# Moving a block inversion from VectorE to GpSimd, and the loads, queries and memory scores around it, in a hybrid decoder trunk

## The chip, the cores and the metric

The kernel runs on one core of a Trainium2 chip. The metric is device time in microseconds of one launch. The kernel before takes 1113.31 us as the median of three runs (1112.72 to 1115.05). The engines are named as in the profile: PE (TensorE), DVE (VectorE), ACT (ScalarE), POOL (GpSimd) and SP (SyncE, which in this kernel only issues transfers). Each engine runs its own instructions strictly in the order in which they stand in its queue; engines wait for each other through semaphores.

## The reference, cut to what matters

Two layers over 512 positions of width 1024. Layer 0 is a gated DeltaNet layer with 6 heads of 128 and a memory attention with 4 heads of 64 over 256 fixed tokens; layer 1 is sliding-window attention with the same kind of memory attention; each layer ends in a SwiGLU block. The change lies in layer 0 only:

```
proj = h @ w_in                                   # h: rms_norm(x)
qkv  = silu(causal_depthwise_conv(proj[..., :2304], conv_w))
q, k = l2_normalize(...), l2_normalize(...)       # 6 heads of 128
lower = where(strict, (k*beta) @ k^T * decay, 0)  # per head and chunk of 64
sol   = triangular_solve(I + lower, [v*beta, k*beta*exp(g)])
intra = q @ k^T * decay
state = state*g_last + k_g^T @ (u - w @ state); o = q_g @ state + intra @ v_new
mem_o = softmax(mem_q @ mem_k^T / 8) @ mem_v
x     = x + concat([gated_norm(o), mem_o]) @ w_out
```

The kernel uses chunks of 128 rather than 64 positions: 4 chunks for each of 6 heads, so 24 lower triangular matrices of 128 x 128 that have to be inverted.

## The kernel before, in words

Activations lie transposed, with 128 features on the partitions and the 512 positions along the row. Each f32 matrix product is made of three passes of a faster kind: weights and activations are both split into a high and a low part (`whi`, `wlo`, `h`, `l`), and `mm3` (L198) issues high by high, high by low and low by high. One projection, that is one tile of 128 outputs of `w_in`, is thus 8 x 3 = 24 matmuls of 128x512 into one PSUM bank `pj`. Its weights come by one SP transfer of 512 KB into `wraw` (`load`, L174 to L178, two buffers), ACT copies them to `whi` (L138) and DVE subtracts to get `wlo` (L151). A weights load therefore waits until the weights two before it have been split.

The function `gdn` is layer 0's mixer. After the keys it forms, per head and chunk, the strictly lower matrix `N`, and sends its 32x32 diagonal blocks (24 matrices x 4 blocks = 96) to DRAM and back, so that they lie as 96 partitions of 1024 numbers. `base_inverse` (L778) inverts all 96 blocks at once by forward substitution: 31 rounds, each a product of a column by a row (`btmp`) and a subtraction from the inverse (`big`), on rectangles of r x w with w = 1 to 31 and r = 32 - w. Each of these 62 instructions needs the one before it. Then ACT writes a turned copy, SP stores both to DRAM (`basex`, `basext`), and SP loads them back as blocks (`X`, 4 loads; `Tt`, 4 loads) into the places that `solve` works on. `solve` starts on PE after the queries and joins the blocks to inverses of 128.

While that runs, PE works on the queries. Six projections give the queries of heads 0 to 5, three by three, in `memory` and the loop after it (L694 to L708). Each is followed by a causal convolution (`conv_tile`: one ACT copy, three DVE instructions into `qv`), an ACT silu, and `query` (L682): four 128x128 products with the keys into a bank `g`, a DVE product into `DT`, a DVE product into `gcr`, an ACT square into `sq`, and an SP store of `sq` to DRAM (`q`). The tile `sq` has one buffer, so the square of a head waits until the store of the head before has landed.

The memory attention of layer 0 is done in two halves (m = 0, 1). `scores` makes eight products of 64x256 (16 matmuls in the profile) into banks `g` and `sc`, DVE takes the maxima, ACT the exponentials into `sm`. `weigh` scales `sm`, turns it on PE into banks `g`, ACT copies these into `pf` (one buffer), and PE multiplies `pf` by the memory values into a bank `sc`. There are two banks `g`, three `sc` and three `pj`.

A scheduler sets the order on each engine from the program's order, the data and its own reckoning of durations; `nosync(a, b)` only makes it put a behind b, without a wait on the chip.

Of the kernel before, what the change touches and what calls it, by code (L numbers as in the profile page):

```python
# [9 lines left out]
F32 = mybir.dt.float32  # L10
# [3 lines left out]
ALU = mybir.AluOpType  # L14
# [4 lines left out]
P = 128  # L19
T = 512  # L20
D = 1024
KD = D // P
H = 6
NC = 4
# [6 lines left out]
BASE = 32  # L31
# [3 lines left out]
LN_EXP = "natural_log_exp_and_others"  # L35
# [49 lines left out]
class Builder:  # L85
# [466 lines left out]
    def gdn(self, gp):  # L552
        nc, a, tc = self.nc, self.a, self.tc
# [29 lines left out]
        for h in range(H):  # L583
            ps = self.begun[h] if h < 3 else None
# [11 lines left out]
            if h == 3:  # L596
                late = self.copied
# [22 lines left out]
        for h in range(H):  # L620
            d = DT[h]
# [36 lines left out]
        self.use(LN_EXP)  # L658
        scores = [self.scores(gp, qm[0], self.memK[0], False)]
        memory_queries(1)  # L660
        X, every_t = self.base_inverse(gp, base_in, known)
        Tt = [every_t[:, h * NC:(h + 1) * NC, :] for h in range(H)]
        for i in range(NH):
            h, c = divmod(i, NC)
            self.copy(kg[h][:, c, :], kg[h][:, c, :], scale=f[:, 2, i:i + 1])

        def memory(m, first, late):

            if m:
                self.use(LN_EXP)  # L670
                scores.append(self.scores(gp, qm[m], self.memK[m], False))
            ps = self.normed(first)
            steps = self.projected(a["win"][first + 1], self.h)
            nxt = [next(steps) for _ in range(2)]
            self.ahead = self.last
            while late:
                query(*late.pop(), self.ahead)
            self.weigh(gp, scores[m], self.memV, m, mq[m], None)
            nxt.extend(steps)
            return ps, nxt[-1]  # L680

# [15 lines left out]
        late = []  # L697
        for h0 in (0, 3):
            ps = memory(h0 // 3, h0, late)
            ts = [self.conv_tile(h0 + n, self.t(gp, [P, T], F32, "qv", 5), ps[n] if n < 2 else None) for n in range(3)]  # L700
            behind = self.last
            self.use(SILU_SIN)
            for h, t in zip(range(h0, h0 + 3), ts):
                self.fn(t, t, AF.Silu)
                if h == 2:
                    late.append((h, t))
                else:
                    query(h, t, behind)  # L708
# [65 lines left out]
    def base_inverse(self, gp, base_in, after):  # L774

        nc = self.nc
        n = NH * NB
        e = BASE * BASE  # L778
        whole = self.t(gp, [P, 4 * T], F32, "big")
        big = lambda i: whole[:n, i * e:(i + 1) * e].rearrange("p (a b) -> p a b", b=BASE)  # L780
        L = big(0)
        nc.sync.dma_start(L.rearrange("p a b -> p (a b)"), base_in.rearrange("n b e -> (n b) e"))
        X = big(1)
        Xf = X.rearrange("p a b -> p (a b)")
        clear = lambda out, value: self.nosync(nc.vector.memset(out, value).ins, after)
        clear(Xf, 0.0)
        clear(Xf[:, ::BASE + 1], 1.0)
        for j in range(BASE - 1):
            r, w = BASE - 1 - j, j + 1
            tmp = self.t(gp, [n, 256], F32, "btmp", 2)[:, :r * w].rearrange("p (i m) -> p i m", m=w)  # L790
            self.tt(nc.vector, tmp, L[:, j, j + 1:].unsqueeze(2).to_broadcast([n, r, w]),
                    X[:, j, :w].unsqueeze(1).to_broadcast([n, r, w]), ALU.mult)
            self.tt(nc.vector, X[:, j + 1:, :w], X[:, j + 1:, :w], tmp, ALU.subtract)
        Xt = big(0)
        self.copy(Xt, X.rearrange("p i m -> p m i"))
        outs = []
        for nm, src in (("basex", X), ("basext", Xt)):
            d = self.t(self.dpool, [NH, NB, BASE * BASE], F32, nm)
            nc.sync.dma_start(d.rearrange("n b e -> (n b) e"), src.rearrange("p a b -> p (a b)"))
            outs.append(d)  # L800
        X64 = self.t(gp, [P, NH, 2 * BASE], F32, "X64")
        clear(X64, 0.0)
        for b in range(NB):
            s = slice(b * BASE, (b + 1) * BASE)
            o = b % 2 * BASE
            nc.sync.dma_start(X64[s, :, o:o + BASE], outs[0][:, b, :].rearrange("n (i m) -> i n m", m=BASE))
        Tt = self.t(gp, [P, NH, P], F32, "Tt")
        clear(Tt, 0.0)
        for b in range(NB):
            s = slice(b * BASE, (b + 1) * BASE)  # L810
            nc.sync.dma_start(Tt[s, :, s], outs[1][:, b, :].rearrange("n (m i) -> m n i", i=BASE))
        return X64, Tt

    def solve(self, gp, N, X64, Tt):
# [93 lines left out]
        return new  # L908


    def scores(self, pool, q, kk, win, sinks=None):

        nc = self.nc
        own = "pt" in self.pbufs
# [5 lines left out]
        for n0 in range(0, NC, 2):  # L920
# [5 lines left out]
            for n in (n0, n0 + 1):  # L926
                ks = slice((n - 1) * P if n else 0, (n + 1) * P) if win else slice(0, ML)
                c0 = P if win and n == 0 else 0
                for b in range(2):
                    self.ahead = self.mm(ps[b][:, n - n0, c0:], q[half[b], n * P:(n + 1) * P], kk[half[b], ks])  # L930
                    if self.valued is not None:

                        self.nosync(self.ahead, self.valued)
                        self.valued = None
            for b in range(2):
                i = b * NC + n0
                if win:
# [813 lines left out]
```

## Time and profile before

| what | value |
|---|---|
| median of three runs | 1113.31 us |
| the profiled execution | 1112.83 us |
| its span, first to last instruction | 1111.1 us |
| busy share of PE, DVE, ACT, POOL | 99%, 84%, 63%, 10% |
| queries, weighing and solve of layer 0 | about 119 to 195 us of the span |
| granted clock | 0.998 |

The profiled execution lies 0.48 us under the median, and 1.73 us of it lie outside the span. A timeline row gives the start in the span, the length, the engine, the line, the operation, the tiles (out<-in), the shapes and how many equal instructions it joins; behind it, in brackets, the engine's idle time before it and what ended that. PE's rows overlap, since matmuls are pipelined: there the distance from one start to the next is the cost. A line can be that of a helper: L144 is every matmul, L151 every two-operand DVE or POOL instruction, L138 every ACT copy.

### The profile page before, as it was taken

The numbers are of one execution on the slowest core, as the hardware profiler recorded it, in microseconds if no ns is written. First come the engines' busy times: TensorE is split into PE (matmuls) and PEld (weight loads), VectorE is DVE, ScalarE is ACT, GpSimd is POOL, SyncE is SP. The second block draws the span as 40 slices with busy tenths as digits, with TensorE's granted clock in tenths as the row PEclk, the third lists the DMA queues.
The fourth block names the chain that finished last, engine by engine and source line by source line (L and its number), as shares of the span: only waits on it lengthen the run. The fifth ranks groups of instructions, "written<-read, shape, count | busy, mean of one in ns | idle before, by whom it ended". The sixth has DMA issues, their size and how long they took to land.

```text
span 1111.1 us, 21262 instructions
## 1 busy us (share of the span) xinstructions
PE 1100.6 (99%) x7957; PEld 998.9 (90%) x7957; DVE 937.0 (84%) x1890; ACT 697.2 (63%) x1470; POOL 105.9 (10%) x129
## 2 busy tenths in 40 slices
PE   9999999999999999999999999999999999999997
PEld 8888778877899999999998777788899999999996
DVE  7685977667899999999997977839999999998964
ACT  7588674466566656665565654866667466655644
POOL 0000000000011121112110000000111111121101
PEclk9999999999999999999999999999999999999999
DMA  8244352234567787778753321114677776778632
GB/s 320 98 151 142 114 142 82 90 98 145 150 173 183 189 190 191 179 184 199 191 147 99 117 74 40 58 58 142 159 176 192 189 195 184 186 198 203 148 86 90
DMA packets 81146, 165.36 MB, mean 149 GB/s; under 512 B 18588, under 2 KB 20148, under 8 KB 81044
## 3 DMA queue, kind: packets, MB, share of 16 engines
q1 hardware_dynamic: 64436, 133.87, 38.0%
q0 software_dynamic: 16320, 29.89, 16.5%
q8 instruction: 62, 1.02, 0.4%
q14 instruction: 40, 0.33, 0.1%
q10 hardware_dynamic: 288, 0.26, 0.1%
HBM read 156.98 MB, written 7.01 MB: 148 GB/s over the span
## 4 chain that ended last, share of the span: by engine, by line
PE 92%; DVE 5%; ACT 1%; issue 1%; DMA 0%; SPq 0%; DVEq 0%; ACTq 0%
PE g L144 54%; PE pj L144 26%; PE sc L144 6%; PE qk L144 3%; PE pt L144 2%; PE pt L148 1%; DVE wlo L151 1%; PE g L148 1%; DVE l L154 1%; DVE big L151 1%; DVE x L151 1%; DMA early<-in_early 0%; DVE fu L151 0%; DVE qv L154 0%; DVE btmp L151 0%
## 5 line engine op out<-in xcount | busy, mean ns | idle before, releaser
L138 ACT ACTIVATE whi<-wraw 128x512 fp32r<-128x512 f32 (+2 forms) x357 | 250.6, 711 | 161.4 <-PE g L144 66.3
L151 DVE TENSOR_TENSOR wlo<-wraw,whi 128x512 fp32r<-128x512 f32 (+2 forms) x357 | 280.5, 793 | 36.8 <-ACT whi L138 31.8
L144 PE MATMUL g<-T,whi 128*128 128x256 f32 x1280 | 228.3, 279 | 0.0
L144 PE MATMUL g<-h,wlo 128*128 128x256 f32 (+1 forms) x780 | 222.7, 285 | 0.6 <-DVE wlo L151 0.6
L144 PE MATMUL g<-l,whi 128*128 128x256 f32 (+1 forms) x780 | 222.6, 285 | 0.0
L144 PE MATMUL g<-h,whi 128*128 128x256 f32 (+1 forms) x780 | 222.4, 285 | 0.0
L144 PEld LDWEIGHTS g<-T,whi 128*128 128x128 f32 x1280 | 194.9, 188 | 0.5 <-DVE fu L154 0.5
L144 PE MATMUL pj<-h,whi 128*128 128x512 f32 (+1 forms) x460 | 182.0, 398 | 0.0
L144 PE MATMUL pj<-l,whi 128*128 128x512 f32 (+1 forms) x460 | 180.4, 393 | 0.4 <-DVE l L154 0.3
L144 PE MATMUL pj<-h,wlo 128*128 128x512 f32 (+1 forms) x460 | 179.8, 391 | 0.0
L144 PE MATMUL g<-T,wlo 128*128 128x256 f32 x640 | 178.5, 279 | 0.0
L144 PEld LDWEIGHTS g<-h,wlo 128*128 128x128 f32 x780 | 146.6, 188 | 2.8 <-DVE wlo L151 1.1
L144 PEld LDWEIGHTS g<-l,whi 128*128 128x128 f32 x780 | 146.6, 188 | 1.9
L144 PEld LDWEIGHTS g<-h,whi 128*128 128x128 f32 x780 | 146.6, 188 | 1.8
L144 PEld LDWEIGHTS g<-T,wlo 128*128 128x128 f32 x640 | 120.3, 188 | 0.0
L144 PEld LDWEIGHTS pj<-h,whi 128*128 128x128 f32 x460 | 86.4, 188 | 20.7 <-issue 4.1
L144 PEld LDWEIGHTS pj<-h,wlo 128*128 128x128 f32 x460 | 86.5, 188 | 18.0 <-issue 0.9
L144 PEld LDWEIGHTS pj<-l,whi 128*128 128x128 f32 x460 | 86.5, 188 | 17.8 <-DVE l L154 1.2
L138 ACT ACTIVATE whi<-ws 128x512 fp32r<-128x512 f32 x112 | 70.1, 626 | 38.9 <-PE g L144 36.8
L151 DVE TENSOR_TENSOR wlo<-ws,whi 128x512 fp32r<-128x512 f32 x112 | 77.1, 689 | 2.9 <-ACT whi L138 2.9
L1394 POOL DMA_DIRECT2D ws<-in_wgu x40 | 35.1, 878 | 414.6 <-DVE l L154 203.9
L138 ACT ACTIVATE fs<-g 128x256 f32<-128x256 f32 x168 | 61.5, 366 | 1.1 <-PE g L144 0.7
(398 smaller groups left out, 1929.6 us busy)
## 6 DMA issues: line engine op xcount, KB each, us to landing
wraw<-in_wgu SPq DMA_DIRECT2D x48, 512.0 KB, 4.0
ws<-in_wgu SPq DMA_DIRECT2D x80, 256.0 KB, 3.6
ws<-in_wgu POOLq DMA_DIRECT2D x80, 256.0 KB, 4.9
wraw<-in_win SPq DMA_DIRECT2D x26, 512.0 KB, 4.0
wraw<-in_wgu SPq DMA_DIRECT2D x40, 256.0 KB, 5.4
wraw<-in_wout SPq DMA_DIRECT2D x16, 512.0 KB, 3.4
ws<-in_wdn SPq DMA_DIRECT2D x32, 256.0 KB, 5.7
wraw<-in_wdn SPq DMA_DIRECT2D x16, 512.0 KB, 3.8
```

Source lines behind the costliest of these rows:

```text
L138: self.copied = self.nc.scalar.activation(out, in_, AF.Copy, **kw).ins
L144: return self.nc.tensor.matmul(out, lhsT, rhs, start=start, stop=stop, skip_group_check=more).ins
L148: return self.nc.tensor.transpose(out, in_, self.ident[:k, :k]).ins
L151: return eng.tensor_tensor(out=out, in0=a, in1=b, op=op).ins
L154: return self.nc.vector.scalar_tensor_tensor(out=out, in0=in0, scalar=scalar, in1=in1, op0=op0, op1=op1).ins
L1394: nc.gpsimd.dma_start(s1, a22, accum_op=ALU.add)
```

## The change

Five things are altered, all in layer 0.

1. The 62 instructions of the block inversion, the turned copy and the two stores go to POOL; before, they stood on DVE, ACT and SP.
2. `base_inverse` ends with the stores. The clearing of `X64` and `Tt` and the eight block loads become a function of their own, `base_blocks`, which is called after the convolution of head 5's query has been issued; its loads stay on SP, and are put behind the load of the sixth query's weights.
3. The second half's `scores` come right behind the first half's weighing, and no longer behind the queries of heads 0 and 1. So ACT no longer changes its table of functions twice in between.
4. The queries of heads 0 and 1 (before: only that of head 2) are put off into the second `memory`: behind the first three of the eight steps of head 3's projection. Head 2's stays behind two steps of head 4's.
5. `scores` gets an argument `after`, which no call uses.

```diff
-        X, every_t = self.base_inverse(gp, base_in, known)
-        Tt = [every_t[:, h * NC:(h + 1) * NC, :] for h in range(H)]
+        outs = self.base_inverse(gp, base_in, known)
...
         def memory(m, first, late):
 
+            steps = self.projected(a["win"][first], self.h)
             if m:
-                self.use(LN_EXP)
-                scores.append(self.scores(gp, qm[m], self.memK[m], False))
-            ps = self.normed(first)
+                nxt = [next(steps) for _ in range(3)]
+                while len(late) > 1:
+                    query(*late.pop(0), self.last)
+            ps = list(steps)[-1]
             steps = self.projected(a["win"][first + 1], self.h)
             nxt = [next(steps) for _ in range(2)]
             self.ahead = self.last
             while late:
                 query(*late.pop(), self.ahead)
             self.weigh(gp, scores[m], self.memV, m, mq[m], None)
+            if not m:
+                scores.append(self.scores(gp, qm[1], self.memK[1], False))
             nxt.extend(steps)
             return ps, nxt[-1]
...
             ps = memory(h0 // 3, h0, late)
-            ts = [self.conv_tile(h0 + n, self.t(gp, [P, T], F32, "qv", 5), ps[n] if n < 2 else None) for n in range(3)]
+            conv = lambda n, ps: self.conv_tile(h0 + n, self.t(gp, [P, T], F32, "qv", 5), ps)
+            ts = [conv(n, ps[n]) for n in range(2)]
+            ts.append(conv(2, None))
             behind = self.last
+            if h0:
+                X, every_t = self.base_blocks(gp, outs, known, self.loaded)
+                Tt = [every_t[:, h * NC:(h + 1) * NC, :] for h in range(H)]
             self.use(SILU_SIN)
             for h, t in zip(range(h0, h0 + 3), ts):
                 self.fn(t, t, AF.Silu)
-                if h == 2:
+                if h < 3:
                     late.append((h, t))
...
-            self.tt(nc.vector, tmp, L[:, j, j + 1:].unsqueeze(2).to_broadcast([n, r, w]),
+            self.tt(nc.gpsimd, tmp, L[:, j, j + 1:].unsqueeze(2).to_broadcast([n, r, w]),
                     X[:, j, :w].unsqueeze(1).to_broadcast([n, r, w]), ALU.mult)
-            self.tt(nc.vector, X[:, j + 1:, :w], X[:, j + 1:, :w], tmp, ALU.subtract)
+            self.tt(nc.gpsimd, X[:, j + 1:, :w], X[:, j + 1:, :w], tmp, ALU.subtract)
         Xt = big(0)
-        self.copy(Xt, X.rearrange("p i m -> p m i"))
+        nc.gpsimd.tensor_copy(Xt, X.rearrange("p i m -> p m i"))
         outs = []
         for nm, src in (("basex", X), ("basext", Xt)):
             d = self.t(self.dpool, [NH, NB, BASE * BASE], F32, nm)
-            nc.sync.dma_start(d.rearrange("n b e -> (n b) e"), src.rearrange("p a b -> p (a b)"))
+            nc.gpsimd.dma_start(d.rearrange("n b e -> (n b) e"), src.rearrange("p a b -> p (a b)"))
             outs.append(d)
+        return outs
+
+    def base_blocks(self, gp, outs, known, after):
+
+        nc = self.nc
+        clear = lambda out, value: self.nosync(nc.vector.memset(out, value).ins, known)
         X64 = self.t(gp, [P, NH, 2 * BASE], F32, "X64")
         clear(X64, 0.0)
         for b in range(NB):
             s = slice(b * BASE, (b + 1) * BASE)
             o = b % 2 * BASE
-            nc.sync.dma_start(X64[s, :, o:o + BASE], outs[0][:, b, :].rearrange("n (i m) -> i n m", m=BASE))
+            self.nosync(nc.sync.dma_start(
+                X64[s, :, o:o + BASE], outs[0][:, b, :].rearrange("n (i m) -> i n m", m=BASE)).ins, after)
...
-            nc.sync.dma_start(Tt[s, :, s], outs[1][:, b, :].rearrange("n (m i) -> m n i", i=BASE))
+            self.nosync(nc.sync.dma_start(
+                Tt[s, :, s], outs[1][:, b, :].rearrange("n (m i) -> m n i", i=BASE)).ins, after)
         return X64, Tt
```

What this makes of the order shows at three places. The first is SP's queue around the block loads. `wraw` are weights loads, `q` the stores of the squares of heads 0, 1 and 2, in this order. Before:

```order
L177 DMA wraw_1826<-in_win 128x1024
L695 DMA q_314_1647<-sq_1645 128x512
L177 DMA wraw_2096<-in_win 128x1024
L695 DMA q_317_1659<-sq_1657 128x512
L799 DMA basex_1442<-big_1344 96x1024
L799 DMA basext_1444<-big_1344 96x1024
L806 DMA X_288_1446<-basex_1442 32x24x32 x4
L811 DMA Tt_1452<-basext_1444 32x24x32 x4
L695 DMA q_337_1749<-sq_1747 128x512
```

And now, with `wraw_1813` the sixth query's weights and `wraw_2094` the first ones for the values:

```order
L177 DMA wraw_1714<-in_win 128x1024
L177 DMA wraw_1813<-in_win 128x1024
L820 DMA X_350_1848<-basex_1442 32x24x32 x4
L826 DMA Tt_1854<-basext_1444 32x24x32 x2
L698 DMA q_325_1686<-sq_1684 128x512
L826 DMA Tt_1854<-basext_1444 32x24x32
L698 DMA q_328_1697<-sq_1695 128x512
L826 DMA Tt_1854<-basext_1444 32x24x32
L177 DMA wraw_2094<-in_win 128x1024
L698 DMA q_335_1736<-sq_1734 128x512
```

The stores of heads 0 and 1 stood ahead of the block loads; now all three stores and the next weights load stand behind the first six or more of the eight block loads.

The second place is ACT's queue around the three squares (`sq`), with the waits that the built program holds; `DMAHW1` and `DMAHW3` on the second and third square are the landings of the stores of the square before, `DMAHW5` that of `wraw_2094`. Before, from the copy of head 1's convolution to the silu of head 2:

```order
L138 ACTIVATE qv_1595<-pj_1519,gains_67 128x512 [waits DMAHW7_49,PE_49]
L132 ACTIVATE qv_1595<-qv_1595 128x512 [waits DVE_49,Activation_49]
L138 ACTIVATE qv_1600<-pj_1607,gains_67 128x512 [waits PE_49]
L693 ACTIVATE sq_1657<-qv_1595 128x512 [waits DMAHW3_49,Activation_49]
L138 ACTIVATE whi_1828<-wraw_1826 128x1024 [waits DMAHW2_49]
L138 ACTIVATE big_1344<-big_1344 96x1024 [waits DVE_49,Pool_49]
L132 ACTIVATE qv_1600<-qv_1600 128x512 [waits DVE_49,Activation_49]
```

And now:

```order
L138 ACTIVATE whi_1815<-wraw_1813 128x1024 [waits DMAHW2_49,PE_49]
L138 ACTIVATE qv_1621<-pj_1628,gains_67 128x512 [waits PE_49]
L132 ACTIVATE qv_1616<-qv_1616 128x512 [waits DVE_49]
L696 ACTIVATE sq_1695<-qv_1616 128x512 [waits DMAHW1_49,Activation_49]
L132 ACTIVATE qv_1621<-qv_1621 128x512 [waits DVE_49]
L696 ACTIVATE sq_1734<-qv_1621 128x512 [waits DMAHW3_49,Activation_49]
L138 ACTIVATE qv_1802<-pj_1667,gains_67 128x512 [waits PE_49]
L138 ACTIVATE whi_2096<-wraw_2094 128x1024 [waits DMAHW5_49]
L138 ACTIVATE pf_1740<-g_1743 128x4x128 [waits PE_49]
L138 ACTIVATE pf_1740<-g_1751 128x4x128 [waits PE_49]
```

Head 1's square now has head 2's silu (`qv_1621`), head 2's square, a weights split and the copies for the second weighing behind it; before, the corresponding copies stood far behind head 1's square.

The third place is PE around the scores of the second half (`qm` against `m`). Before they followed the products of heads 0 and 1 (`qv` by `kn`):

```order
L144 MATMUL g_1638<-qv_1590,kn_131_697 128x128 x4
L144 MATMUL g_1650<-qv_1595,kn_132_703 128x128 x4
L144 MATMUL sc_1682<-m_63_412,qm_248_1310 128x256
L144 MATMUL sc_1683<-m_63_412,qm_248_1310 128x256
L144 MATMUL g_1668<-m_63_412,qm_248_1310 128x256 x2
L144 MATMUL sc_1682<-m_63_412,qm_248_1310 128x256
L144 MATMUL g_1669<-m_63_412,qm_248_1310 128x256 x2
L144 MATMUL sc_1683<-m_63_412,qm_248_1310 128x256
```

Now they stand around the last product of the first weighing (`sc` from `pf`):

```order
L148 MATMUL g_1548<-consts_66,sm_1276 128x128 x4
L144 MATMUL sc_1579<-m_63_412,qm_248_1310 128x256
L144 MATMUL g_1565<-m_63_412,qm_248_1310 128x256
L144 MATMUL sc_1515<-pf_1537,m_64_414 64x256 x2
L144 MATMUL sc_1515<-pf_1537,m_65_416 64x256 x2
L144 MATMUL g_1566<-m_63_412,qm_248_1310 128x256
L144 MATMUL g_1565<-m_63_412,qm_248_1310 128x256
L144 MATMUL g_1566<-m_63_412,qm_248_1310 128x256
L144 MATMUL sc_1580<-m_63_412,qm_248_1310 128x256
L144 MATMUL sc_1579<-m_63_412,qm_248_1310 128x256
L144 MATMUL sc_1580<-m_63_412,qm_248_1310 128x256
```

Between the last turning (`g_1548`) and the product that needs its copy there stood four matmuls of a projection; now two of the scores stand there. The projections' matmuls themselves are the same, 71 of them from here to the product of head 2's query (`g_1740` before, `g_1727` now).

More of the change, by code (lines that the diff above doesn't have):

```diff
@@ L908, in scan_step, with scores @@
         return new
-    def scores(self, pool, q, kk, win, sinks=None):
+    def scores(self, pool, q, kk, win, sinks=None, after=None):
         nc = self.nc
@@ L934, in scores @@
                         self.valued = None
+                    if after is not None:
+                        self.nosync(self.ahead, after)
+                        after = None
             for b in range(2):
```

## The prediction

> **What bounds the kernel now.** I read the head of the page first, then the chain of waits, then the stretch of the change in windows.
>
> ```profile
> span 1111.1 us, 21262 instructions
> PE 92%; DVE 5%; ACT 1%; issue 1%; DMA 0%; SPq 0%; DVEq 0%; ACTq 0%
> 140.00:160.00 20.00, 19.58 (x99) 15.88 (x99) 16.96 (x42) 15.12 (x32) 0.00 (x0) 1.00 0.56 136
> 160.00:180.00 20.00, 20.00 (x202) 16.08 (x201) 13.26 (x21) 10.55 (x16) 0.00 (x0) 1.00 0.18 64
> ```
>
> 92% of the chain that ended last is PE, and in the stretch of the change PE (first busy number of a window) has one visible gap. So DVE's time is worth nothing here by itself: only what makes PE wait, or stop waiting, moves the end. PE's timeline shows where it loses time, and gives the prices of its pieces:
>
> ```profile
> 117.44 1.14 PE L144 MATMUL g<-m,qm 64*128 64x256 f32 x8
> 118.41 1.03 PE L144 MATMUL sc<-m,qm 64*128 64x256 f32 x8
> 119.37 0.50 PE L144 MATMUL pj<-h,whi 128*128 128x512 f32 x1
> ...
> 135.09 0.48 PE L144 MATMUL pj<-l,whi 128*128 128x512 f32 x1
> ...
> 136.19 1.08 PE L144 MATMUL sc<-pf,m 128*64 128x256 f32 x8
> ...
> 147.88 0.70 PE L144 MATMUL sc<-m,qm 64*128 64x256 f32 x4
> 149.00 1.13 PE L144 MATMUL g<-m,qm 64*128 64x256 f32 x4 [0.42 <-DVE DT L151]
> ...
> 151.84 0.50 PE L144 MATMUL pj<-h,whi 128*128 128x512 f32 x1
> ...
> 158.79 1.06 PE L144 MATMUL g<-qv,kn 128*128 128x128 f32 x8
> ...
> 162.93 1.08 PE L144 MATMUL sc<-pf,m 128*64 128x256 f32 x8
> ```
>
> The first half's scores took 119.37 - 117.44 = 1.93 us from start to start. The second half's, the same 16 matmuls, took 151.84 - 147.88 = 3.96 us: they wait for banks `g` that DVE has yet to empty (the 0.42 <-DVE DT). From 151.84 to 158.79 PE does 30 projection matmuls, 0.232 us each with the switches.
>
> **The change part by part.**
>
> *Scores moved.* Out of their old place they free 3.96 us. In the new one, two of the eight pairs of matmuls fill the time (135.09 to 136.19) in which ACT copies `pf` and four projection matmuls ran before; the other six pairs cost 6/8 of 1.93 = 1.45 us, and the four displaced matmuls come later, 4 x 0.232 = 0.93 us. Gain 3.96 - 2.38 = 1.6 us. It can't be under 0 unless the pairs wait for their banks as before, nor over 3.96 - 1.93 = 2.0. The two changes of ACT's table that go free only ACT. The products of heads 0 and 1 now have 59 projection matmuls and the six pairs ahead of them; I count them at nothing.
>
> So PE would come to head 2's product (`g_1727`), before at 158.79, at 157.2, if nothing holds it.
>
> *Inversion on POOL.* DVE is freed of 62 instructions:
>
> ```profile
> 111.55 0.19 DVE L151 TENSOR_TENSOR btmp<-big 96x31 f32<-96x31 f32 x1 [1.53 <-DMA big<-basein]
> ...
> L151 DVE TENSOR_TENSOR btmp<-big x31: 177/354/421, 111.6 to 148.2; 96x31 f32<-96x31 f32 x2, 96x60 f32<-96x60 f32 x2, 96x87 f32<-96x87 f32 x2, 96x112 f32<-96x112 f32 x2
> L151 DVE TENSOR_TENSOR big<-big,btmp x31: 176/355/420, 111.8 to 148.9; 96x31 f32<-96x31 f32 x2, 96x60 f32<-96x60 f32 x2, 96x87 f32<-96x87 f32 x2, 96x112 f32<-96x112 f32 x2
> ```
>
> About 62 x 0.355 = 22 us, hidden behind PE, so worth nothing. On POOL the chain cannot begin before 111.55 either, the landing of its input. POOL's prices come from elsewhere in the program:
>
> ```profile
> L151 POOL TENSOR_TENSOR T<-T,ws 128x256 f32<-128x256 f32 x4 | 2.8, 732 | 57.5 <-ACT ws L132 57.5
> L1509 POOL MEMSET sinT<- 128x512 f32 x1 | 0.5, 525 | 180.5 <-PE sc L144 180.5
> L283 POOL MEMSET ones<- 128x128 f32 x1 | 0.2, 204 | 0.3 <-POOLq L1742 0.3
> L1742 POOL MEMSET const-float32-0.0<- 128x1 f32 x1 | 0.1, 98 | 0.2 <-issue 0.2
> ```
>
> The rectangles hold w(32 - w) numbers, 5,456 over w = 1 to 31, twice: 10,912. The two memsets give (525 - 204)/384 = 0.84 ns a number and 97 ns fixed. With that fixed part, 732 ns at 256 numbers is 2.48 ns a number: 62 x 0.097 + 10,912 x 0.00248 = 33.1 us. If nothing is fixed it is 2.86 ns, 31.2 us; if all is fixed, 62 x 0.732 = 45.4 us. On top, each instruction waits for the one before; the four in the row were in independent pairs, so this is not shown. I add POOL's shortest row, 0.098 us, 62 times: 6.1 us (between 0 and that). I take 33.1 + 6.1 = 39.2, near the middle of 31.2 and 51.5. The chain ends at 150.75.
>
> *Turned copy, stores, loads.* These rows price them (ACT, SP, and transfers with size and us to landing):
>
> ```profile
> 149.13 2.01 ACT L138 ACTIVATE big<-big 96x1024 f32<-96x1024 f32 x1 [0.36 <-DVE big L151]
> ...
> 119.67 14.99 SPq L177 DMA_DIRECT2D wraw<-in_win  x3
> ...
> 149.07 0.33 SPq L799 DMA_DIRECT2D basex<-big  x1
> ...
> 152.07 2.37 SPq L806 DMA_DIRECT2D X<-basex  x4
> 154.54 2.64 SPq L811 DMA_DIRECT2D Tt<-basext  x4
> ...
> mv<-kt POOLq DMA_DIRECT2D x2, 128.0 KB, 3.9
> mk<-kt POOLq DMA_DIRECT2D x2, 128.0 KB, 2.4
> ...
> q<-sq SPq DMA_DIRECT2D x6, 256.0 KB, 2.0
> ...
> wraw<-in_win SPq DMA_DIRECT2D x26, 512.0 KB, 4.0
> ```
>
> The copy on POOL: 0.95 us by the memsets, 2.6 by the two-operand row; ACT's own 2.0 lies between, I take it: 152.8. POOL issues the first store after the copy. SP's took 149.07 to 152.07, 3.0 us, until its loads went; POOL's small stores landed in 2.4 and 3.9. I take 3.9 (2.4 to 4.9, one us more for three times the size): `basex` lands at **156.7**; `basext`, half a us behind, is covered by the four `X` loads.
>
> The sixth weights load stands at about 134.7 (the last of the three from 119.67 on), so SP then stands still before the first `X` load until 156.7. Queued behind it: two `Tt` loads, the store of head 0's square, and more. Four `X` loads 2.37, two `Tt` loads 2.64/2 = 1.32: the store is issued at 160.4 and lands, 2.0 later, at 162.4. Only then can ACT make the second square, since `sq` has one buffer, and behind it in ACT's queue stands head 2's silu, for which PE waits. ACT's groups in the stretch, mean ns second last number but one:
>
> ```profile
> L138 ACT ACTIVATE whi<-wraw 128x1024 fp32r<-128x1024 f32 x6 | 6.3, 1055 | 6.0 <-PE pj L144 5.9
> L138 ACT ACTIVATE pf<-g 128x512 f32<-128x512 f32 x4 | 2.2, 598 | 1.7 <-PE sc L144 1.3 <-PE g L148 0.4
> L138 ACT ACTIVATE qv<-pj,gains 128x512 f32<-128x512 f32 x3 | 2.0, 668 | 0.0
> L132 ACT ACTIVATE qv<-qv 128x512 f32<-128x512 f32 x3 | 1.9, 631 | 5.5 <-DVE qv L154 5.5
> L693 ACT ACTIVATE sq<-qv 128x512 f32<-128x512 f32 x2 | 1.2, 625 | 0.0
> ```
>
> Square 0.63 and silu 0.63: PE goes on at 163.7 instead of 157.2, **6.5 us** of waiting. Then the second wait. Head 1's store is issued at 163.05, lands at 165.05; the next weights load goes behind it and the last `Tt` load (0.66), at 164.05, and lands 4.0 later at 168.05. ACT: head 2's square to 165.7, a copy to 166.35, then it waits for the weights, splits them to 169.1, copies `pf` twice (1.1) to 170.2; PE's second weighing starts at 170.35. PE got there at 163.7 + (162.93 - 158.79) - 5 x 0.232 = 166.7, since five of the eight projection matmuls that stood between stand later now: **3.7 us** more. Everything downstream shifts with PE.
>
> Sum: 6.5 + 3.7 - 1.6 = +8.6. In general, with B the landing of `basex`, the change costs B - 148.1; below 148.1 nothing but the gain stays. On the profiled execution's own 1112.83 us (span and 1.73 around it; 0.48 under the median) that is **1121.4 us**. Ends: B = 111.55 + 31.2 + 0.95 + 2.4 = 146.1 gives -1.6, 1111.2; B = 111.55 + 51.5 + 2.6 + 4.9 = 170.55 gives +22.4, 1135.
>
> A rule of the Trainium skill bears on the waits (TensorE: Matmul & The Clock Gate, Part 1): after an idle window of about 3.4 us PE runs at half clock until it has been busy as long. By an estimate from that figure some 1.7 us would come on top; the granted clock of both windows above is 1.00, and nowhere in this stretch does PE wait so long, so no trace here shows it.
>
> **The rivals.**
>
> *POOL in time (not slower).* If the 62 instructions end by 142 (B under 148.1), the forecast's waits vanish and the moved scores' 1.6 us stay: 1111.2 us. It needs 0.49 us an instruction, wait included. For it: 176 numbers on the mean against 256 in POOL's row, and that the scheduler put the loads ahead of the stores, so it reckoned with an early landing. Against: 732 ns scaled by size alone is already 0.50. It decides from B = 148.1 downwards. Where B lies between 146 and 150.3 the time is within 2.2 us of before.
>
> *POOL and DVE in each other's way.* During the chain DVE keeps two-operand work on SBUF:
>
> ```profile
> L151 DVE TENSOR_TENSOR wlo<-wraw,whi 128x1024 fp32r<-128x1024 f32 x5 | 6.1, 1216 | 0.0
> L151 DVE TENSOR_TENSOR gcr<-gcr,qv 128x512 f32<-128x512 f32 x2 | 1.4, 693 | 0.1
> ```
>
> If POOL stands still for each, 7.5 us come on top: B = 164.2, +16.1, 1128.9 us. Nothing in this trace has both at work on SBUF operands for long, so it speaks neither way. The Trainium skill states such an exclusion (SBUF — State Buffer, section "SBUF: two separate sides"): a DVE instruction with two SBUF inputs and a reading GpSimd instruction take a shared port pair whole, and the later one blocks.
>
> *The moved queries wait instead.* Heads 0 and 1 could hold PE where they stand now, since their silu follows eight exponentials and a table load on ACT; a us or so, inside the range.
>
> **How the numbers follow.** The forecast (slower, B from 150.3 to about 161) has 0.55; POOL held up by DVE, or its chain near its upper end, 0.19; within the bound 0.14, most of it POOL nearly in time; POOL in time with more gained than I can price, 0.12. A measurement of this kernel can tell 0.2%, 2.2 us, from no change. So: faster 0.12, same 0.14, slower 0.74. The likeliest case's own range is 1115 to 1126. The range for 8 in 10 leaves out little below (the gain is bounded near 1.6 to 2) and runs on to the held-up case: 1111.5 to 1133.
>
> **What would show it.** POOL's row for `btmp` at 0.55 to 0.75 us from start to start and its end near 151; the first `X` load on SP near 157 with nothing issued since 135; the second `sq` on ACT waiting for a transfer, some 10 us; PE idle twice, before `g<-qv,kn` and before `sc<-pf`, about 6 and 4 us; the 16 score matmuls in one piece near 136. Wrong would be: POOL's chain done before 142, PE without idle time before head 2's product, or ACT never waiting for the store.

## The result and the profile after

The changed kernel takes 1126.24 us (median of 4, 1125.69 to 1127.34) against 1113.03 us of the kernel before on the same chip: 1.18% slower, the 95% interval of the ratio 1.0106 to 1.0130. That is 13.2 us by the medians and 13.4 by the two profiled spans, where 8.6 was forecast. The head of the page after, with the chain by engine:

```profile
span 1124.5 us, 21262 instructions
PE 87%; DVE 4%; POOL 4%; DMA 2%; issue 1%; ACT 1%; SPq 0%; DVEq 0%; POOLq 0%; ACTq 0%
```

POOL, which the chain before didn't have, now holds 4% of it, transfers 2% instead of 0. PE's timeline of the same stretch:

```profile
156.85 0.39 PE L144 MATMUL pj<-h,wlo 128*128 128x512 f32 x1
166.64 2.08 PE L144 MATMUL g<-qv,kn 128*128 128x128 f32 x8 [9.40 <-ACT qv L132]
...
171.68 1.12 PE L148 MATMUL g<-consts,sm 128*128 128x128 f32 x4 [1.26 <-DVE DT L151]
...
173.45 1.12 PE L148 MATMUL g<-consts,sm 128*128 128x128 f32 x4 [0.23 <-ACT pf L138]
174.50 1.73 PE L144 MATMUL sc<-pf,m 128*64 128x256 f32 x8
...
177.67 1.08 PE L144 MATMUL sc<-pf,m 128*64 128x256 f32 x8
```

Head 2's product starts at 166.64 (before 158.79), after 9.4 us of waiting for ACT's silu; the second weighing's product at 174.50 (before 162.93). Why ACT is late stands in SP's timeline and in ACT's:

```profile
119.64 13.23 SPq L177 DMA_DIRECT2D wraw<-in_win  x3
159.11 2.25 SPq L820 DMA_DIRECT2D X<-basex  x4
161.46 1.03 SPq L826 DMA_DIRECT2D Tt<-basext  x2
162.59 0.48 SPq L698 DMA_DIRECT2D q<-sq  x1
163.11 0.43 SPq L826 DMA_DIRECT2D Tt<-basext  x1
166.09 0.34 SPq L698 DMA_DIRECT2D q<-sq  x1
166.47 0.43 SPq L826 DMA_DIRECT2D Tt<-basext  x1
167.00 0.57 SPq L177 DMA_DIRECT2D wraw<-in_win  x1
```

```profile
150.61 0.62 ACT L132 ACTIVATE qv<-qv 128x512 f32<-128x512 f32 x1
165.44 0.63 ACT L696 ACTIVATE sq<-qv 128x512 f32<-128x512 f32 x1 [14.21 <-DMA q<-sq]
165.97 0.61 ACT L132 ACTIVATE qv<-qv 128x512 f32<-128x512 f32 x1
168.25 0.63 ACT L696 ACTIVATE sq<-qv 128x512 f32<-128x512 f32 x1 [1.67 <-DMA q<-sq]
...
171.86 1.06 ACT L138 ACTIVATE whi<-wraw 128x1024 fp32r<-128x1024 f32 x1 [2.40 <-DMA wraw<-in_win]
```

SP issues nothing between the last weights load of the first row and 159.11, when the stored inverse has landed. The store of head 0's square, behind six block loads, goes at 162.59, and ACT's second square waits 14.21 us for it, with head 2's silu (165.97) behind it. The next weights load goes at 167.00; ACT can split it at 171.86. POOL's timeline, and DVE's beside it:

```profile
111.22 0.23 POOL L151 TENSOR_TENSOR btmp<-big 96x31 f32<-96x31 f32 x1 [71.29 <-DMA big<-basein]
...
113.48 0.37 POOL L151 TENSOR_TENSOR btmp<-big 96x112 f32<-96x112 f32 x1
113.93 1.29 POOL L151 TENSOR_TENSOR big<-big,btmp 96x112 f32<-96x112 f32 x1
...
148.53 1.24 POOL L151 TENSOR_TENSOR btmp<-big 96x112 f32<-96x112 f32 x1
149.84 0.42 POOL L151 TENSOR_TENSOR big<-big,btmp 96x112 f32<-96x112 f32 x1
...
153.57 0.25 POOL L151 TENSOR_TENSOR big<-big,btmp 96x31 f32<-96x31 f32 x1
153.88 2.10 POOL L803 COPY big<-big 96x1024 f32<-96x1024 f32 x1
155.93 0.54 POOL L807 DMA_DIRECT2D basex<-big  x1
```

```profile
113.50 1.43 DVE L151 TENSOR_TENSOR wlo<-wraw,whi 128x1024 fp32r<-128x1024 f32 x1 [3.51 <-ACT whi L138]
...
148.22 1.31 DVE L151 TENSOR_TENSOR wlo<-wraw,whi 128x1024 fp32r<-128x1024 f32 x1
```

The chain ran from 111.22 to 153.82. The same shapes (96x112) appear twice: 0.37 and 0.42 us alone, 1.24 and 1.29 beside a DVE subtraction of two SBUF operands, each time until just after DVE has ended (113.93 + 1.29 = 115.22, DVE's end 114.93). The clock in windows of 2 us (the granted share is the number ahead of the last two of a row):

```profile
166.00:168.00 2.00, 1.36 (x6) 1.36 (x7) 0.69 (x1) 0.58 (x2) 0.00 (x0) 0.50 0.47 147
...
174.00:176.00 2.00, 2.00 (x11) 0.94 (x9) 0.86 (x2) 1.03 (x2) 0.00 (x0) 0.54 0.40 94
176.00:178.00 2.00, 2.00 (x16) 1.32 (x14) 0.00 (x0) 1.18 (x2) 0.00 (x0) 1.00 0.91 289
```

PE came back from its wait at half clock and kept it for some 9 us. So the second wait shows as only 1.26 + 0.23 us of idle time: the rest of it is filled with work at half clock.

### The profile page after: what moved, and what is told of

It reads as the page before. It is cut to its first block, busy times and chain, and to the rows that moved or that the text cites. A ratio compares the mean times of both kernels' runs of the same rounds, so it can differ in the third digit from the quotient of the medians.

```text
span 1124.5 us, 21262 instructions
## 1 busy us (share of the span) xinstructions
PE 1104.5 (98%) x7957; PEld 1002.1 (89%) x7957; DVE 922.6 (82%) x1828; ACT 693.1 (62%) x1467; POOL 145.7 (13%) x194
## 4 chain that ended last, share of the span: by engine, by line
PE 87%; DVE 4%; POOL 4%; DMA 2%; issue 1%; ACT 1%; SPq 0%; DVEq 0%; POOLq 0%; ACTq 0%
PE g L144 52%; PE pj L144 24%; PE sc L144 5%; PE qk L144 3%; PE pt L144 2%; POOL btmp L151 2%; POOL big L151 2%; DVE wlo L151 1%; PE pt L148 1%; DVE fu L151 1%; PE g L148 1%; DVE x L151 1%; DVE l L154 1%; DMA early<-in_early 1%; DMA wraw<-in_win 0%
```

## The experiments

Single executions of one kernel differ by 3 us and more (before: 1111.87 to 1115.72), and in the profiled ones up to 2.6 us of that lie behind 303 us. So each trace is also read by a **stretch**: from PE's first matmul of the first scores (117.44 before) to the first turning of the values behind the solve (196.23 before), 78.79 us. The last column is the next 107 us, up to the first row sum of the first gate projection (303.17 before). All are starts in PE's timeline, differences to before.

| kernel | median us (before) | ratio, 95% | stretch | next |
|---|---|---|---|---|
| changed | 1126.24 (1113.03) | 1.0106 to 1.0130 | +13.68 | 0.0 |
| 15 rounds left out | 1110.78 (1113.45) | 0.9967 to 0.9988 | -1.18 | 0.0 |
| 6 rounds left out | 1119.07 (1113.00) | 1.0043 to 1.0071 | +7.40 | 0.0 |
| low parts from one operand | 1128.06 (1112.71) | 1.0110 to 1.0146 | +12.09 | +1.6 |
| three squares | 1127.30 (1113.45) | 1.0108 to 1.0141 | +14.98 | 0.0 |
| loads on POOL | 1115.83 (1113.45) | 1.0015 to 1.0037 | +1.30 | +1.6 |
| the same, three squares | 1112.91 (1112.71) | 0.9986 to 1.0006 | -0.85 | +1.6 |
| loads behind head 2's store | 1114.78 (1112.71) | 1.0003 to 1.0022 | +0.87 | +1.6 |
| the same, three squares | 1113.77 (1112.71) | 0.9991 to 1.0011 | -1.58 | +1.6 |
| the same, other bank | 1111.79 (1113.00) | 0.9981 to 0.9998 | -1.47 | 0.0 |
| scores and queries only | 1115.77 (1113.45) | 1.0007 to 1.0030 | +1.60 | -0.1 |
| scores only | 1117.63 (1113.00) | 1.0025 to 1.0053 | +5.05 | -0.1 |
| inversion on DVE | 1119.06 (1113.00) | 1.0040 to 1.0071 | +3.57 | +1.6 |

### Is the lateness of POOL's chain the whole loss?

```diff
-        for j in range(BASE - 1):
+        for j in range(16):
```

> The changed kernel with 16 of the 31 rounds of the inversion left out of the program's end (rounds 17 to 31 are not made, so the inverses are not whole; nothing else differs). POOL's chain then ends near 134 instead of 153.8, and the stored blocks land near 139. Theory (the lateness of POOL's chain is the whole loss; the cost is its landing less 148): no wait is left, 1111.2 us (1110.5 to 1112.5). Rival (the loads' new place, the POOL copy and stores or the later queries cost by themselves): 1114 us or more.

It held (`range(16)` makes 16 rounds, so 15 are left out and not 16): SP's first block load goes at 138.84, PE has no wait over 0.3 us in the stretch, and the kernel is 0.12 to 0.33% faster than before. The new places of loads, copy, stores and queries cost at most 0.4 us of the stretch (-1.18 here against -1.58 in the best stretch below); lateness costs the rest. The second kernel has `range(25)` in this line:

> The changed kernel with the last 6 of the 31 rounds of the inversion left out (the inverses are not whole); SP's and ACT's queues are as in the changed kernel. POOL's chain ends near 146.1 instead of 153.8, the copy at 148.2, and the stored inverse lands near 151.4. Theory (cost = landing less 148.1): 3.3 us above before, 1116.3 us (1115.3 to 1117.3); PE's longest wait is then near 2 us and its granted clock stays 1.00 in the 20 us after it. Rival (the landing's lateness costs more than one for one even when small): 1117.5 to 1119 us. Second rival (a late landing of this size is hidden): 1110.5 to 1112 us, as with 15 rounds left out.

This one missed: 6.1 us by the medians instead of 3.3, close to the rival's time (more than one for one), and the clock did not stay at 1.00. The first block load went at 150.93, as foreseen. PE's timeline of that kernel, and then of the one with 15 rounds left out:

```profile
160.27 0.40 PE L144 MATMUL pj<-l,whi 128*128 128x512 f32 x1
163.66 0.66 PE L148 MATMUL g<-consts,sm 128*128 128x128 f32 x4 [2.99 <-DVE DT L151]
...
165.43 1.12 PE L148 MATMUL g<-consts,sm 128*128 128x128 f32 x4 [0.73 <-ACT pf L138]
166.48 1.98 PE L144 MATMUL sc<-pf,m 128*64 128x256 f32 x8
...
171.13 1.08 PE L144 MATMUL sc<-pf,m 128*64 128x256 f32 x8
```

```profile
159.62 0.60 PE L148 MATMUL g<-consts,sm 128*128 128x128 f32 x4
160.23 1.08 PE L144 MATMUL sc<-pf,m 128*64 128x256 f32 x8
...
162.76 1.08 PE L144 MATMUL sc<-pf,m 128*64 128x256 f32 x8
```

From the last turning to the weighing's second product PE needs 171.13 - 165.43 = 5.70 us instead of 162.76 - 159.62 = 3.14: **2.56 us** lost at half clock, after a longest wait of only 3 us. The windows of 2 us of the first of the two show the clock:

```profile
162.00:164.00 2.00, 0.34 (x3) 0.34 (x4) 1.96 (x4) 0.16 (x1) 0.00 (x0) 1.00 0.86 245
164.00:166.00 2.00, 1.27 (x7) 0.81 (x6) 1.33 (x2) 2.00 (x4) 0.00 (x0) 0.56 0.46 184
...
170.00:172.00 2.00, 2.00 (x11) 0.88 (x10) 0.00 (x0) 0.14 (x1) 0.00 (x0) 0.73 0.02 6
```

In the changed kernel it is 177.67 - 173.45 = 4.22, a loss of 1.08. The shorter wait lost more to the clock, because in the changed kernel PE spent most of its slow time (166.64 to 173.45) in work and waits that the late weights hid anyway. The loss is that of the profiled execution, the slowest of four (1121.84 us at a mean clock of 0.995); the fastest took 1118.09 at 0.998, the mean clock of before, so after a wait of this length the clock does not fall alike each time.

With that taken off, the cost follows the landing one for one in these two kernels. Counted from the start of the scores (117.15 and 116.91), the first block load stands at 41.96 and 34.02; the stretch less the clock's loss is 12.60 and 4.84: 7.76 us for 7.94. Both give cost = landing - 29.3, in the changed kernel's own time landing - 146.4, where the prediction had 148.1 in the time of before, which is 147.8 in the changed kernel's (its scores start 0.29 us earlier).

### What makes POOL's chain late?

```diff
-            self.split(raw[:, s], hi[:, s], lo[:, s], eng or self.weng)
+            if getattr(self, "lone", False):
+                self.copy(hi[:, s], raw[:, s])
+                self.low = self.nc.vector.tensor_scalar(out=lo[:, s], in0=raw[:, s], scalar1=0.5, scalar2=None, op0=ALU.mult).ins
+            else:
+                self.split(raw[:, s], hi[:, s], lo[:, s], eng or self.weng)
...
```

The flag `lone` is set for layer 0's gate, memory and query projections alone. In the changed kernel eight of POOL's 62 instructions are too long, six beside a weights subtraction (0.86 to 0.92 us each) and two beside a product into `gcr` (0.32 and 0.43), 6.0 us in all; the expectation counts five and two.

> The changed kernel, but the low parts of the weights of layer 0's gate, memory and query projections are made by DVE from one SBUF operand (raw weights times 0.5) instead of two (raw less high part); the low parts are therefore not the right numbers. Theory (POOL stands still while DVE works with two SBUF operands): of POOL's seven long instructions during the chain, the five beside a weights subtraction (about 0.87 us too long each, 4.4 us) become as short as their neighbours, the two beside the products into gcr stay; the chain ends near 149.4 instead of 153.8, and since every us of it counts, the time is 1121.9 us (1121.0 to 1123.0). Rival (POOL's long instructions have another cause): chain's end within 1 us of 153.8 and 1125.5 to 1127 us.

About half of it came. The chain took 39.6 us instead of 42.6 and ended at 151.1, 2.7 us earlier, and the stretch shrank by 1.6. DVE's and POOL's rows of that kernel:

```profile
117.06 0.69 DVE L189 TENSOR_SCALAR wlo<-wraw 128x1024 fp32r<-128x1024 f32 x1 [3.67 <-PE pj L144]
```

```profile
117.19 0.91 POOL L151 TENSOR_TENSOR btmp<-big 96x175 f32<-96x175 f32 x1
```

The one-operand form takes DVE 0.69 us instead of 1.2 to 1.5, and POOL is held up for just that shorter time (0.91 us; the same shape takes 0.49 alone). So the long instructions follow DVE, as the theory says, but the new form holds POOL up too, which the expectation had excluded. The median, 1128.06, didn't fall to the 1121.9 foreseen, and lies above the rival's range too: a wait at 298 us, told below, gave 1.6 back, and the 800 us behind it were 1.2 slower than in the changed kernel's profiled execution.

### Where does the wait sit, and what stands behind it?

```diff
-            sq = self.t(gp, [P, T], F32, "sq", 1)
+            sq = self.t(gp, [P, T], F32, "sq", 3)
```

> The changed kernel with three buffers for the squares instead of one, so ACT's second square no longer waits for the store of the first; SP's queue is as in the changed kernel. Theory (two waits in series behind the late block loads): the first wait of PE, 9.4 us ahead of head 2's product at 166.64, goes; PE gets there at about 156.9. The second stays: the weights load behind the block loads goes at about 164.2 instead of 167.00, so the second weighing starts at about 171.2 instead of 174.50. Time 1122.8 us (1122.0 to 1124.0). Rival (the one buffer of squares is the whole loss): 1111 to 1113 us, and PE without a wait before the second weighing.

Neither theory had this: nothing was gained. ACT's rows, and the one of PE with its wait:

```profile
156.28 0.67 ACT L138 ACTIVATE qv<-pj,gains 128x512 f32<-128x512 f32 x1
171.63 1.06 ACT L138 ACTIVATE whi<-wraw 128x1024 fp32r<-128x1024 f32 x1 [14.69 <-DMA wraw<-in_win]
```

```profile
173.23 1.11 PE L148 MATMUL g<-consts,sm 128*128 128x128 f32 x4 [13.07 <-ACT pf L138]
```

The first wait went, as foreseen, and the whole of it came back at the second: the weights, issued at 165.73 (1.3 us earlier than in the changed kernel), landed at 171.63 (0.2 earlier), and PE idled 13 us in one piece and then worked at half clock through the whole weighing. The theory had the weights issued 2.8 us earlier; but the first block load went 0.8 us later from the start of the scores, and the weights took 5.9 us to land instead of 4.9. Why they did stays open. The two waits hang on one late queue, so the later end alone decides.

```diff
-            self.nosync(nc.sync.dma_start(
+            self.nosync(nc.gpsimd.dma_start(
                 X64[s, :, o:o + BASE], outs[0][:, b, :].rearrange("n (i m) -> i n m", m=BASE)).ins, after)
...
-            self.nosync(nc.sync.dma_start(
+            self.nosync(nc.gpsimd.dma_start(
                 Tt[s, :, s], outs[1][:, b, :].rearrange("n (m i) -> m n i", i=BASE)).ins, after)
```

> The changed kernel with the eight block loads issued by POOL, behind its own two stores, instead of SP; the squares keep one buffer. SP then sends the stores of the squares and the next weights as soon as they are there. Theory: both waits go, and the moved scores' gain is left: 1111.2 us (1110.5 to 1112.5), the solve on PE at about 173.7 with the blocks landed before it. Rival (the blocks are simply too late, whichever queue loads them): the solve waits, 1115 us or more. Second rival: POOL makes these loads of many short rows slowly, 2 us each or more; then the last lands at about 177 and the time is about 1114 us.

With the line of the three squares above added:

> The block loads on POOL and three buffers for the squares. With the loads on POOL alone ACT still waited 2.2 us for the store of head 1's square, with the split of the next weights and the copies for the second weighing behind it, and PE lost about 2.3 us at that weighing. Theory: with the buffers that goes, the solve starts at 173.7 instead of 176.0, and the time falls by 2.3 us from 1115.8 to 1113.5 (1111.0 to 1114.3). Rival (PE's small waits there come from the weights load that shares the transfer engines, not from ACT's order): no change, 1115 to 1116.5.

With SP free, 12.4 us of the stretch's loss are gone at once. The first of the two missed its time all the same, 1115.83 instead of 1111.2: 2.9 us of that are in the stretch (+1.30 where the scores' gain alone would give -1.6), and 1.6 us are the wait at 298 us, told below. The second held, at 1112.91. Now the three buffers help (2.15 us): what had been worthless behind the stalled queue decides when the queue moves. POOL's own loads go slowly, 12.9 us from the first issue to the last in the first kernel (the last at 172.79, landing at 176.56), but PE's first product with `Tt` stands at 181.95 there, so they were in time.

```diff
-            nc.sync.dma_start(q2[h], sq)
+            self.stored = nc.sync.dma_start(q2[h], sq).ins
...
-                X, every_t = self.base_blocks(gp, outs, known, self.loaded)
+                X, every_t = self.base_blocks(gp, outs, known, self.stored)
```

> The changed kernel with the block loads still on SP, but put behind the store of head 2's square instead of behind the sixth weights load. The stores of heads 0 to 2 and the next two weights loads then stand ahead of them. Theory: PE's two waits go, the same small wait of ACT for head 1's store stays: 1114.0 us (1112.5 to 1115.5). Rival (something now queued behind the late loads, the eighth weights load or the store of head 3's square, takes the place of what was freed): 1117 us or more, with ACT waiting for one of these two transfers.

Again with three squares added:

> As the run with the loads behind the store of head 2's square, with three buffers for the squares. Theory: all waits of the stretch go and the moved scores' gain is left: 1111.5 us (1110.5 to 1113.0). Rival (loads of blocks and weights in flight together delay the weights, whatever the queue): 1113.5 us or more.

Both stretches came as expected: putting the late loads behind the stores takes 12.8 us off the changed kernel's stretch, and with three squares the moved scores' gain of 1.6 us is there in full. The first time held (1114.78); that of the second, 1113.77, was still 2.3 us over its forecast and would fit its rival, but the trace has no wait of PE in the stretch. The list of PE's waits shows where 1.6 us of it are:

```profile
PE pj L144 <- DVE x L151: 1.3, 1, 1.3
```

This wait, at the first gate projection near 298 us, stands in all kernels with +1.6 in the last column and in no other. The order of PE's tiles there is that of the others; the built programs differ in that the projection's first matmul also waits for DVE, which a tile gets with the bank that it takes over, as the next run bears out.

```diff
-        bank = lambda m: self.bank(("pj", "pj", "pt")[m % 3] if begun else "g" if m % 4 == 3 else "pj")
+        bank = lambda m: self.bank(("pj", "pj", "pt")[m % 3] if begun else "sc" if m == 3 else "g" if m == 7 else "pj")
```

> The block loads behind the store of head 2's square and three buffers for the squares, as run before; and in the output projection the fourth of eight tiles takes a bank sc instead of g. PE's order is otherwise unchanged. In the run without this, PE had the moved scores' gain of 1.6 us up to 290 us, and then lost 1.6 us at 298 us, where the first matmul of the first gate projection waits for DVE's last addition into x; by the built program this bank change takes that wait off. Theory: 1113.8 less 1.6 = 1112.2 us or less, about 1 us under before (1110.8 to 1112.6), and PE without a wait for x at 298 us. Rival (the wait comes back at the next projection, since DVE is behind there): no change, 1113 to 1114 us.

The wait is gone, and at 1111.79 us this is the one kernel with a whole inversion that lies under before: by 0.02 to 0.19%, at the edge of what can be told, and 1.3% under the changed one. A gain in one stage was eaten some 100 us later, by a bank that fell differently.

### Is the freed DVE worth anything?

The prediction said no. Three kernels keep the inversion on DVE with the scores moved. The first has copy, stores and loads as before the change, so that of the changed kernel only the scores and the later queries are left:

```diff
-            self.tt(nc.gpsimd, tmp, L[:, j, j + 1:].unsqueeze(2).to_broadcast([n, r, w]),
+            self.tt(nc.vector, tmp, L[:, j, j + 1:].unsqueeze(2).to_broadcast([n, r, w]),
...
-            self.tt(nc.gpsimd, X[:, j + 1:, :w], X[:, j + 1:, :w], tmp, ALU.subtract)
+            self.tt(nc.vector, X[:, j + 1:, :w], X[:, j + 1:, :w], tmp, ALU.subtract)
...
-        nc.gpsimd.tensor_copy(Xt, X.rearrange("p i m -> p m i"))
+        self.copy(Xt, X.rearrange("p i m -> p m i"))
...
-            nc.gpsimd.dma_start(d.rearrange("n b e -> (n b) e"), src.rearrange("p a b -> p (a b)"))
+            nc.sync.dma_start(d.rearrange("n b e -> (n b) e"), src.rearrange("p a b -> p (a b)"))
...
         outs = self.base_inverse(gp, base_in, known)
+        X, every_t = self.base_blocks(gp, outs, known, None)
...
```

> Only the moved scores and the later queries: the inversion on DVE, the turned copy on ACT, stores and block loads on SP as before the change. Theory: the scores give 1.6 us and no wait comes in, since the inversion ends near 149 and the store of head 0's square stands ahead of the block loads: 1111.4 us (1110.8 to 1113.0). Rival (the later queries cost of themselves, the silu of heads 0 and 1 being late behind the exponentials): 1113.5 to 1115 us, with PE waiting for a silu before the products of head 0 or 1.

The second has the old place of the queries of heads 0 and 1 as well:

```diff
-                if h < 3:
+                if h == 2:
                     late.append((h, t))
...
```

> Before with the moved scores alone: inversion, copy, stores and loads as before, and the queries of heads 0 and 1 in their old place. Theory (of the run with moved scores and later queries, the loss against the forecast comes from the queries, which stand behind the copy on ACT and behind DVE's convolutions): 1112 us (1111 to 1113). Rival (the loss comes from DVE, which holds the inversion and the moved maxima at the same time): 1113.5 to 1116 us.

The third is the changed kernel with the first two lines of the first alone:

> The changed kernel with the 62 instructions of the inversion back on DVE; the copy and the two stores stay on POOL, the block loads behind the sixth weights load on SP. Here the scheduler puts the stores of heads 0 and 1 and two weights loads ahead of the block loads. Theory: no wait for the blocks; what is left is what the run with the moved scores alone had (a wait for a silu and DVE's copies in the solve) and the wait for x at 298 us: 1115.5 us (1113.5 to 1117). Rival (the POOL copy and stores or the place of the loads cost by themselves): 1120 us or more.

All three lost and came out over their forecasts (1115.77 for 1111.4, 1117.63 for 1112, 1119.06 for 1115.5), and my theory of the first two fell: the later queries aren't the cost, for without them it is worse. The waits are behind DVE and ACT; a row of the first kernel, a row and a window of the second, and two rows of the third:

```profile
179.13 0.21 PE L144 MATMUL sc<-Tt,big 32*32 32x32 f32 x1 [1.32 <-DVE big L860]
```

```profile
151.72 1.63 PE L144 MATMUL g<-qv,kn 128*128 128x128 f32 x7 [1.92 <-ACT qv L132]
```

```profile
152.00:154.00 2.00, 2.00 (x10) 1.90 (x10) 1.59 (x3) 1.41 (x3) 0.00 (x0) 0.50 0.95 222
```

```profile
149.37 2.85 DVE L151 TENSOR_TENSOR wlo<-wraw,whi 128x1024 fp32r<-128x1024 f32 x1
```

```profile
149.01 2.13 POOL L803 COPY big<-big 96x1024 f32<-96x1024 f32 x1 [108.00 <-DVE big L151]
```

In the first PE waits for DVE's copies in the solve, 1.7 us in all, and 0.7 for a silu. In the second it waits 1.9 us for a silu that stands behind the turned copy on ACT, and 2.2 for the same copies; and the clock fell to half for 3.4 us behind the wait of 1.92 us, from 152.0 to 155.4, which by half of that time cost some 1.7 us more. In the third, DVE's subtraction, 1.2 us alone, takes 2.85, as long as POOL's copy runs beside it (to 151.14); and ACT waits 3.1 us for the store of a square, with copies into `pf` behind it for which PE waits 1.9. The third kernel's order of stores and loads on SP is nearest to that of the loads behind head 2's store with one square (+0.87), and it lies 2.7 us of the stretch higher. So in the orders tried here moving the scores pays only with DVE or ACT relieved. How much of it is DVE's own time and how much the copy on ACT and the order that the scheduler chose isn't separated.

## Why the prediction was right, and where it was off

**The mechanism** came point by point: SP silent until the inverse has landed, the second square waiting for the store behind the block loads, head 2's silu behind it, then the weights. The sign and the range held, though the measured 1126.24 lies just above the likeliest case's own range; the forecast, 1121.4, was 4.8 us too low by the profiled spans. Of the signs, PE's two idle pieces came as 9.4 and 1.5 us and not as 6 and 4, since half clock filled the second. The terms:

*Scores moved, 1.6 us.* Right: -1.47 and -1.58 us of the stretch where nothing else waits.

*The chain on POOL, 39.2 us.* It took 42.6, by two errors of opposite sign that partly cancel, which was luck. Eight instructions were held up by DVE for 6.0 us in all. That was put down as a rival with 7.5 us, and should have been a term of the sum, since the diff shows two-operand work on both engines. Without it 36.6 are left, 2.6 under the forecast: the undisturbed rows grow from 0.23 us (product) and 0.25 (subtraction) at 31 numbers to 0.62 and 0.68 at 255, so about 0.18 us are fixed and 1.7 to 1.9 ns come with each number, where I had 0.1 and 2.48, and the pause between dependent instructions is 0.08 us where I had 0.1. The rule of the Trainium skill (SBUF — State Buffer, section "SBUF: two separate sides") was borne out in both directions, POOL held by DVE and DVE by POOL's copy. The same page of the Trainium skill, in its section "Who interferes with whom", names `tensor_scalar` as able to take the shared ports; the one-operand form of 0.69 us agrees, beside which POOL took 0.91 us instead of 0.49.

*Copy and store, 2.0 + 3.9 us.* 2.1 and 3.2. So the inverse landed at 159.1 instead of 156.7: **2.4 us** of the error.

*The first wait, 6.5 us.* 9.6 (166.64 instead of 157.08, one matmul after the last projection's start); 2.4 by the landing, 0.8 by the store, which took 2.8 us to land instead of 2.0.

*The second wait.* Seen from the landing the weights load was issued 0.54 us later than reckoned, and landed 4.86 us after its issue instead of 4.0: **1.4 us**. This is why the zero point of the formula is 146.4 and not 147.8 (148.1 in the time of before). The formula also doesn't fit its own floor: landing - 148.1 reaches the gain of -1.6 only at 146.5, so the waits don't vanish at 148.1 as the prediction says. No run lies in between. That the first wait is only a part of the second's path, so that taking it off alone gives nothing, wasn't seen.

*The clock.* I left it out of the sum because no row of before showed it. It cost **1.1 us** in the profiled execution (0.43 in the turnings, 0.64 behind), and 2.4, 1.4 and 1.1 make 4.9, near the 4.8 that were missing. The clock fell to half also after waits of 2.99 us (6 rounds left out) and 1.92 us (scores only). The Trainium skill (TensorE: Matmul & The Clock Gate, Part 1) states that an idle window of some 3.4 us halves the clock; the wait of 9.4 us agrees, the two shorter ones show that less is enough here. The estimate of 1.7 us from its figure lies between the 1.1 here and the 2.6 of the run with 6 rounds left out; but the half clock lasted 9 us behind the wait and not 3.4, and most of it was hidden.

*DVE's freed 22 us, worth nothing.* Not borne out in company with the moved scores: with the inversion on DVE every kernel tried lost 1.6 to 5 us of the stretch, though not all of that is shown to be DVE's. It couldn't be seen in the windows of before, where DVE was ready in time for another order of work.

The rival of POOL in time (1111.2 us) is what the run with 15 rounds left out shows: 1110.78. The rival of the moved queries waiting for their silu didn't happen in the changed kernel.

## What to carry to other kernels

A transfer that waits for a slow producer holds up everything behind it in its issuing queue, so read which stores and loads stand there and who waits for them; moving it behind them can be worth as much as making the producer faster (here -1.58 us of the stretch with POOL as slow as ever, -1.18 with 15 rounds left out). Where two waits hang on one late event, taking off the earlier one alone may give nothing. And compare a stage by starts in the stage itself as well as by the whole time, for an order changed here may cost or give a wait in another place.

## What was not expected of the hardware

- POOL and DVE hold each other up for whole instructions: POOL some 0.87 us too long beside DVE's subtraction of 1.2 to 1.5 us, DVE 1.6 us too long beside POOL's 2.1 us copy. Beside DVE instructions that read one operand from PSUM (`mq0l<-sc,mq0h`, from 137.79 on) POOL's rows of 240 and 247 numbers stayed at 0.59 to 0.70 us.
- PE's clock fell to half after waits of 3.0 and 1.9 us. The wait of 3.0 us cost more at half clock (2.6 us) than one of 9.4 (1.1), since in the second case other waits covered the slow work.
- Eight loads of short rows issued by POOL took 12.9 and 14.1 us from the first issue to the last, 0.7 to 1.5 us apart with pauses of up to 4.8 us from one to the next; SP issued the same eight in 4.0 to 5.4 us where nothing stood between them.
